# A norm's transposed rows kept in PSUM until VectorE splits them, and a normalisation cut at column 511

## The chip, the cores and the metric

The kernel runs on one core of a Trainium2 chip. The metric is device time in microseconds (us), taken as a median over runs. The engines are TensorE (PE, with its weight loads PEld), VectorE (DVE), ScalarE (ACT), GpSimd (POOL), and SyncE (SP), which issues the transfers. They read and write SBUF, the large on-chip memory, and PSUM, where matmuls accumulate in banks of 512 float32 columns.

## The reference

Two transformer-like layers run over 512 tokens, 256 of them context and 256 latent, with rows of 1024 numbers (D). Layer 0 mixes tokens by a gated delta rule, layer 1 by differential attention; a gated feed-forward network (SwiGLU) follows each. Every one of the four sub-layers is closed by a norm over a row:

```
x = LN(alpha * x + gate * sublayer(x * (1 + scale) + shift))
LN(x) = (x - mean(x)) * rsqrt(mean((x - mean(x))^2) + 1e-5) * g + b
```

`gate`, `scale` and `shift` come from a condition vector and are constant over the tokens of a stream. Only the latent half of the result is returned.

## The kernel before

**Tiles.** The 512 tokens are four tiles `t` of 128 rows (0 and 1 context, 2 and 3 latent). `x` (named `big` in the profile) holds a tile with tokens on the 128 partitions and 1024 columns. A matmul needs the features on the partitions, so each normalised tile is transposed by PE in eight blocks of 128 x 128.

**Products.** All products are made from float32 values that are split in two parts: a rounded one (`hh` of activations, `wh` or `wxh` of weights) and the rest (`hl`, `wl`, `wxl`). Each product is three matmuls: hi x hi, hi x lo, lo x hi (`mm3`). The rest is value minus rounded value, an instruction with two sources (`tt`, line 410), which DVE or POOL may do. The rounded part is a cast by ACT (`cp`, line 424) or DVE (line 425).

**A norm.** `resid` (from line 1417) adds a sub-layer's output, times its gate, to `x` and collects statistics (`bn_stats`, line 1430). `norm` (line 1433) turns them into mean and 1/sqrt by a chain of small operations on one column (`sm`), and writes the normalised row to `n`: DVE takes columns 0 to 511 (`ts`, line 416), ACT 512 to 1023 (`act`, line 437), in parallel. `ln` (line 1450) then starts two threads `to_hT` (line 1458), one for each half row `b`:

1. four transposes of `n` into a PSUM bank `pt` (line 463; banks `wb`, `wc`, `o`);
2. four scale-and-shift operations, out of `pt` into an SBUF buffer `hfb` of 512 columns (named `w` in the profile, as the buffers of the feed-forward network are), each on DVE or ACT; the bank is then free;
3. `hh`, the cast of `hfb`, on ACT or DVE;
4. `hl`, `hfb` minus `hh`, on POOL or DVE; the buffer is then free.

The matmuls of the next sub-layer take `hh` and `hl` from there. A third thread, `ln_x`, multiplies `n` by g and adds b on POOL (`big<-n,lnr`, `big<-big,lnr`), for the next residual.

Three sets of norms go through `to_hT`: LN0 (behind the layer-0 mixer, four tiles, about 465 to 490 us of the span), LN1 (behind the layer-0 feed-forward network, four tiles, about 840 to 873) and LN2 (behind the attention, tiles 2 and 3, about 1069 to 1097). That makes 10 norms and 20 half rows. The last norm of the kernel goes straight to the output and is not touched.

**Order.** No order is written by hand. A planner (class `Sched`) runs when the kernel is built: every thread is a generator with a rank, and each operation gets a planned start from a cost model (`cost`, line 396) and from the engine, buffers and events it needs. `Alt` offers an operation to two engines; the planner takes the one that would end first, with a penalty on DVE set by `spare` (`LNW`, line 76). `shared` (line 404) marks operations that the planner lets exclude each other between DVE and POOL: all of POOL's, and those of DVE with no PSUM source and either two sources or more than one column out. Where it plans PE idle for over 1 us, `warm` (line 526) puts in matmuls on a tile of ones. Each engine runs its list in order.

Of the kernel before, what the change touches and what calls it, by code (L numbers as in the profile page):

```python
# [13 lines left out]
ALU = mybir.AluOpType  # L14
# [360 lines left out]
def trunk_kernel(ctx: ExitStack, tc: tile.TileContext, A: dict, out: bass.AP, dbg=None, stop=None):  # L375
# [11 lines left out]
    def fs(ap):  # L387
        n = 1
        for s in ap.shape[1:]:
            n *= s  # L390
        return n

    isps = lambda *a: any(x.space == PSUM for x in a)
    isap = lambda x: not isinstance(x, (int, float)) and x is not None

    def cost(e, out, srcs, scal=(), one=False):
        n, p = fs(out), sum(1 for x in scal if isap(x))
        if e == "v":
            return ((n / 2 if one and not isps(out, *srcs) else n) + 66 + 58 * p) / 0.96
        if e == "s":  # L400
            return 0.833 * n + (50 if isps(*srcs) else 93) + 93 * p
        return 259 + 3.33 * n if p else 150 + (0.84 * n + 180 if one else 2.1 * n)

    def shared(op, srcs, out=None):

        op.port = op.eng == "g" or (op.eng == "v" and not isps(*srcs) and (len(srcs) > 1 or not isps(out) and fs(out) > 1))
        return op

    def tt(o, a, b, op, e="v"):
        return shared(Op(e, cost(e, o, (a, b)), lambda: E[e].tensor_tensor(o, a, b, op), o, a, b), (a, b))  # L410

    def tta(o, a, b, op):
        return Alt([tt(o, a, b, op, "v"), tt(o, a, b, op, "g")])

    def ts(o, a, s1, s2, o0, o1=None, e="v"):
        f = lambda: E[e].tensor_scalar(o, a, s1, s2, o0, o1) if o1 is not None else E[e].tensor_scalar(o, a, s1, s2, o0)  # L416
        return shared(Op(e, cost(e, o, (a,), (s1, s2), True), f, o, a), (a,), o)

    def stt(o, a, s, b, o0, o1):
        return shared(Op("v", cost("v", o, (a, b), (s,)), lambda: V.scalar_tensor_tensor(o, a, s, b, o0, o1), o, a, b), (a, b))  # L420
# [6 lines left out]
    def cpa(o, a):  # L427
        return Alt([cp(o, a, "s"), cp(o, a, "v")])

    def act(o, a, f, scale=1.0, bias=None, accum=None):  # L430
        kw = {}
        if bias is not None:
            kw["bias"] = bias
        if accum is not None:
            kw["accum_out"] = accum
        c = cost("s", o, (a,), (scale, bias)) + (95 if accum is not None else 0)
        return Op("s", c, lambda: S.activation(o, a, f, scale=scale, **kw), o, a)  # L437

    def spare(alt, wait):

        for op in alt:
            if op.eng == "v":
                op.wait = wait
        return alt

    def dve(o, n, f, *aps):
        return Op("v", (n + 66) / 0.96, f, *aps)
# [13 lines left out]
    def tr(o, a):  # L461
        k = a.shape[0]
        return Op("pe", 110.0, lambda: T.transpose(o, a, ident[0:k, 0:k]), o)  # L463
# [52 lines left out]
    hl = const([P, KT, 512], "hl", F32R)  # L516
    hhf = hh.bitcast(F32)
# [25 lines left out]
    def event(*k):  # L543
        e = ev.setdefault(k, Event())
        e.name = k
        return e
# [15 lines left out]
    def rsqrt(x, n):  # L562

        yb = yield Alloc(SM)
        hb = yield Alloc(SM)
        mb = yield Alloc(SM)
        y, xh, m = yb[:, 0:n], hb[:, 0:n], mb[:, 0:n]
        yield ts(y.bitcast(I32), x.bitcast(I32), 1, None, ALU.logical_shift_right)
        yield Par([ts(y.bitcast(I32), y.bitcast(I32), -1, 0x5F3759DF, ALU.mult, ALU.add),
                   ts(xh, x, -27.0 / 1024.0, None, ALU.mult)])  # L570

        if n == 1:

            zb = yield Alloc(SM)
            z = zb[:, 0:1]
            yield ts(m, y, y, x, ALU.mult, ALU.mult)
            yield ts(z, m, -10.0 / 3.0, m, ALU.add, ALU.mult)
            yield ts(m, z, 5.0, y, ALU.add, ALU.mult)
            yield ts(z, m, m, xh, ALU.mult, ALU.mult)
            yield ts(y, z, 9.0 / 16.0, m, ALU.add, ALU.mult)  # L580
            yield Free(hb, mb, zb)
            return yb
        yield tt(m, y, y, ALU.mult)
        yield tt(m, m, x, ALU.mult)
        yield stt(m, m, -10.0 / 3.0, m, ALU.add, ALU.mult)
        yield stt(y, m, 5.0, y, ALU.add, ALU.mult)
        yield tt(m, y, y, ALU.mult)
        yield tt(m, m, xh, ALU.mult)
        yield stt(y, m, 9.0 / 16.0, y, ALU.add, ALU.mult)
        yield Free(hb, mb)  # L590
        return yb
# [748 lines left out]
    n = 0  # L1340
# [92 lines left out]
    def norm(i, t, stats, done):  # L1433

        yield Wait(*done)
        mv = yield Alloc(SM)
        yield dve(mv, 12, lambda: V.bn_aggr(mv[:, 0:2], stats[:, 0:2, :]))
        yield ts(mv[:, 1:2], mv[:, 1:2], 1e-5, None, ALU.add)
        rs = yield from rsqrt(mv[:, 1:2], 1)
        n = yield Alloc(TNN)  # L1440
        x = xs["x"]
        a, b = slice(0, 512), slice(512, 1024)
        nb = mv[:, 2:3]
        yield ts(nb, mv[:, 0:1], -1.0, rs[:, 0:1], ALU.mult, ALU.mult)
        yield Par([ts(n[:, a], x[:, t, a], mv[:, 0:1], rs[:, 0:1], ALU.subtract, ALU.mult),
                   act(n[:, b], x[:, t, b], AF.Identity, rs[:, 0:1], nb)])
        yield Free(mv, rs, stats)
        return n

    def ln(i, t, stats, done, keep):  # L1450
        n = yield from norm(i, t, stats, done)
        left = [2 + keep]
        for b in range(2):
            spawn(to_hT(i, t, b, n, left), RK_LN + (RK_T[t] if i == 2 else t))
        if keep:
            spawn(ln_x(i, t, n, left), RK_LNX[i] + t)

    def to_hT(i, t, b, n, left):
        r = 1 if t < 2 else 0
        ab = yield Wait(event("fold", i))  # L1460
        w_ = LNW3[i] if t == 3 else LNW[i]
        pt = yield Alloc(*YP)
        hfb = yield Alloc(W5)
        hf = hfb.t.rearrange("p (j n) -> p j n", j=4)
        if i < 2 and t < 3:
            yield Later(LN_SLACK)
        for j in range(4):
            kt = 4 * b + j
            yield tr(pt[:, P * j:P * j + P], n[:, P * kt:P * kt + P])
        ops = []  # L1470
        for j in range(4):
            kt = 4 * b + j
            o, p, sa, sb = hf[:, j, :], pt[:, P * j:P * j + P], ab[:, 0, kt, r:r + 1], ab[:, 1, kt, r:r + 1]
            ops.append(spare(Alt([ts(o, p, sa, sb, ALU.mult, ALU.add), act(o, p, AF.Identity, sa, sb)]), w_[0]))
        yield Par(ops)
        yield Free(pt)
        c, k4 = slice(P * t, P * t + P), slice(4 * b, 4 * b + 4)
        yield spare(cpa(hh[:, k4, c], hf), w_[1])
        yield spare(tta(hl[:, k4, c], hf, hhf[:, k4, c], ALU.subtract), w_[2])
        yield Free(hfb)  # L1480
        left[0] -= 1
        if left[0] == 0:
            yield Free(n)
        yield Set(event("hTb", i, t, b))
        if used(("hT", i, t), 2):
            yield Set(event("hT", i, t))
        if used(("fold", i), 8 if i < 2 else 4):
            yield Free(ab)
# [13 lines left out]
    def used(k, n):  # L1502

        seen[k] = seen.get(k, 0) + 1
        return seen[k] == n
# [633 lines left out]
    LNR, TNN, W5 = xt("lnr", [P, 2, D], 1), xt("n", [P, D], 2), xt("w5", [P, 512], NW5)  # L2139
# [174 lines left out]
```

## Time and profile before

| | |
|---|---|
| median of 3 runs | 1284.76 us (1284.17 to 1285.11) |
| the profiled execution, device time | 1284.39 us |
| span in its profile | 1282.6 us |
| mean granted PE clock | 0.994 |
| PE busy | 1239.9 us, 97% |
| DVE busy | 891.3 us, 69% |
| ACT busy | 575.8 us, 45% |
| POOL busy | 322.5 us, 25% |

The span runs from the first to the last instruction; the device time holds 1.8 us around it. A row such as `L416 DVE TENSOR_SCALAR n<-big,sm,sm` is an instruction of line 416 on DVE, which writes `n` from `big` and two scalars `sm`; buffer numbers are left out. Times are us unless marked ns. What stands in square brackets is how long the engine was idle before an instruction, and what released it.

### The profile page before, as it was taken

How to read it: one execution, taken by the hardware profiler on the slowest of the kernel's cores; microseconds unless marked ns; L12 is line 12 of the kernel's file. 1: busy time of each engine (PE TensorE's matmuls, PEld its weight loads, DVE VectorE, ACT ScalarE, POOL GpSimd, SP SyncE). 2: the span in 40 equal slices, each digit the busy share in tenths (PEclk: the TensorE clock that was granted, in tenths of full speed). 3: DMA queues.
4: the chain of work that ended last, by engine and by line, in shares of the span. 5: the costliest groups of instructions: out<-in, count | busy, mean ns of one | idle time of the engine just before them, and what ended most of it. 6: DMA issues, size and time to landing. Idle time of an engine off the chain costs nothing.

```text
span 1282.6 us, 24147 instructions
## 1 busy us (share of the span) xinstructions
PE 1239.9 (97%) x9576; PEld 1018.9 (79%) x9576; DVE 891.3 (69%) x2036; ACT 575.8 (45%) x1295; POOL 322.5 (25%) x190
## 2 busy tenths in 40 slices
PE   9999899999999999999999999999999998999997
PEld 6576678788787787888888888879878866999986
DVE  3298859698783776888378562475998978655546
ACT  2258657667644435222112322145545444444431
POOL 0013212123222148222101123134122236322200
PEclk9999999999999999999999999999999999999999
DMA  9423312011111743555256563224223155755550
GB/s 367 150 78 137 133 43 76 19 51 51 35 51 61 252 140 133 196 174 180 97 172 209 189 198 104 81 85 144 91 87 124 53 200 182 237 188 184 181 181 33
DMA packets 54753, 171.58 MB, mean 134 GB/s; under 512 B 5744, under 2 KB 14064, under 8 KB 53872
## 3 DMA queue, kind: packets, MB, share of 16 engines
q1 hardware_dynamic: 54640, 170.04, 39.6%
q8 instruction: 75, 1.23, 0.4%
q14 instruction: 38, 0.31, 0.1%
HBM read 168.97 MB, written 1.05 MB: 133 GB/s over the span
## 4 chain that ended last, share of the span: by engine, by line
PE 77%; DVE 15%; ACT 5%; issue 2%; DMA 0%; DVEq 0%; SPq 0%
PE pj L459 32%; PE wa L459 18%; PE wc L459 11%; PE wb L459 6%; PE o L459 6%; DVE acc L420 2%; DVE sm L416 1%; DVE sm L420 1%; PE pj L536 1%; ACT jk L437 1%; PE wc L463 1%; DVE sm L410 1%; DVE hl L410 1%; DVE wl L410 1%; ACT N L424 1%
## 5 line engine op out<-in xcount | busy, mean ns | idle before, releaser
L424 ACT CAST wh<-w 128x1024 fp32r<-128x1024 f32 (+1 forms) x131 | 136.9, 1046 | 207.5 <-PE wa L459 54.8
L459 PE MATMUL pj<-hl,wh 128*128 128x512 f32 (+1 forms) x592 | 219.3, 371 | 0.0
L459 PE MATMUL pj<-hh,wh 128*128 128x512 f32 (+1 forms) x592 | 218.1, 368 | 0.6 <-DVE acc L420 0.6
L410 POOL TENSOR_TENSOR wl<-w,wh 128x1024 fp32r<-128x1024 f32 (+1 forms) x40 | 97.3, 2432 | 385.7 <-ACT wh L424 337.1
L459 PE MATMUL pj<-hh,wl 128*128 128x512 f32 (+1 forms) x512 | 187.5, 366 | 0.0
L459 PEld LDWEIGHTS pj<-hh,wh 128*128 128x128 f32 x592 | 112.5, 190 | 15.7 <-issue 1.1
L459 PEld LDWEIGHTS pj<-hl,wh 128*128 128x128 f32 x592 | 112.2, 190 | 14.5 <-issue 0.7
L410 DVE TENSOR_TENSOR wl<-w,wh 128x1024 fp32r<-128x1024 f32 x52 | 63.5, 1222 | 64.1 <-ACT wh L424 62.7
L459 PEld LDWEIGHTS pj<-hh,wl 128*128 128x128 f32 x512 | 97.3, 190 | 10.6 <-issue 0.2
L459 PE MATMUL wa<-hl,wh 128*128 128x256 f32 (+2 forms) x288 | 96.5, 335 | 0.0
L459 PE MATMUL wa<-hh,wh 128*128 128x256 f32 (+2 forms) x288 | 96.0, 334 | 0.0
L420 DVE SCALAR_TENSOR_TENSOR adaE<-w,sT,adaE 128x512 f32<-128x512 f32 x89 | 73.2, 859 | 5.3 <-DMA w<-in_adaw_dram 4.7
L424 ACT CAST wh<-wx 128x1024 fp32r<-128x1024 f32 x36 | 37.8, 1049 | 58.0 <-PE pj L459 28.1
L420 DVE SCALAR_TENSOR_TENSOR acc<-pj,cst,acc 128x510 f32<-128x510 f32 (+1 forms) x80 | 59.3, 742 | 5.9 <-ACT acc L437 5.0
L459 PE MATMUL wa<-hh,wxl 128*128 128x512 f32 (+1 forms) x176 | 61.7, 350 | 0.0
L459 PE MATMUL pj<-hh,wxl 128*128 128x512 f32 (+1 forms) x176 | 60.9, 346 | 0.0
L459 PEld LDWEIGHTS wa<-hh,wh 128*128 128x128 f32 (+1 forms) x288 | 54.4, 189 | 6.0
L459 PEld LDWEIGHTS wa<-hl,wh 128*128 128x128 f32 (+1 forms) x288 | 54.0, 188 | 6.0
L410 POOL TENSOR_TENSOR hidl<-w,hidh 128x512 fp32r<-128x512 f32 x20 | 29.2, 1462 | 108.1 <-ACT hidh L424 108.1
L410 POOL TENSOR_TENSOR wxl<-w,wh 128x1024 fp32r<-128x1024 f32 x13 | 31.5, 2428 | 82.1 <-ACT wh L424 50.5
L459 PE MATMUL wa<-hh,wl 128*128 128x256 f32 (+2 forms) x152 | 49.9, 328 | 0.0
L410 POOL TENSOR_TENSOR h1l<-fth,h1h 128x256 fp32r<-128x256 f32 x20 | 29.4, 1472 | 77.8 <-ACT h1h L424 77.8
(664 smaller groups left out, 3242.8 us busy)
## 6 DMA issues: line engine op xcount, KB each, us to landing
w<-in_adaw_dram SPq DMA_DIRECT2D x71, 512.0 KB, 4.2
w<-in_wgu_dram SPq DMA_DIRECT2D x59, 512.0 KB, 4.5
w<-in_wd_dram SPq DMA_DIRECT2D x31, 512.0 KB, 3.8
w<-in_wdn_dram SPq DMA_DIRECT2D x26, 512.0 KB, 3.8
wx<-in_adaw_dram SPq DMA_DIRECT2D x17, 512.0 KB, 3.9
w<-in_wo_dram SPq DMA_DIRECT2D x15, 512.0 KB, 4.9
wx<-in_wgu_dram SPq DMA_DIRECT2D x15, 512.0 KB, 4.2
wx<-in_wd_dram SPq DMA_DIRECT2D x10, 512.0 KB, 3.9
```

What stands on the lines that cost most here:

```text
L410: return shared(Op(e, cost(e, o, (a, b)), lambda: E[e].tensor_tensor(o, a, b, op), o, a, b), (a, b))
L416: f = lambda: E[e].tensor_scalar(o, a, s1, s2, o0, o1) if o1 is not None else E[e].tensor_scalar(o, a, s1, s2, o0)
L420: return shared(Op("v", cost("v", o, (a, b), (s,)), lambda: V.scalar_tensor_tensor(o, a, s, b, o0, o1), o, a, b), (a, b))
L424: return Op("s", cost("s", o, (a,)), lambda: S.copy(o, a), o, a)
L437: return Op("s", c, lambda: S.activation(o, a, f, scale=scale, **kw), o, a)
L459: return Op("pe", c, lambda: T.matmul(o, lhsT=l, rhs=r, start=start, stop=stop), o)
L463: return Op("pe", 110.0, lambda: T.transpose(o, a, ident[0:k, 0:k]), o)
L536: T.matmul(t[:, 0:P], lhsT=ones, rhs=ones, start=True, stop=True)
```

## The change

`to_hT` no longer takes the SBUF buffer. The scale-and-shift operations write back into the PSUM bank, in place. `hh` is cast from the bank and `hl` is computed from the bank and `hh`, now always on DVE (before, 16 of the 20 were on POOL and 4, those of LN2, on DVE). The bank is freed after `hl`. `norm` cuts a row at column 511, so DVE does 511 columns and ACT 513. The planner's cost model takes a DVE operation with one SBUF source as twice as fast, and as excluding POOL, only where its width is even.

```diff
@@ cost, shared
-            return ((n / 2 if one and not isps(out, *srcs) else n) + 66 + 58 * p) / 0.96
+            return ((n / 2 if one and n % 2 == 0 and not isps(out, *srcs) else n) + 66 + 58 * p) / 0.96
...
-        op.port = op.eng == "g" or (op.eng == "v" and not isps(*srcs) and (len(srcs) > 1 or not isps(out) and fs(out) > 1))
+        op.port = op.eng == "g" or (op.eng == "v" and not isps(*srcs) and (len(srcs) > 1 or not isps(out) and fs(out) % 2 == 0))
@@ norm
-        a, b = slice(0, 512), slice(512, 1024)
+        a, b = slice(0, 511), slice(511, 1024)
@@ to_hT
         pt = yield Alloc(*YP)
-        hfb = yield Alloc(W5)
-        hf = hfb.t.rearrange("p (j n) -> p j n", j=4)
+        hf = pt.t.rearrange("p (j n) -> p j n", j=4)
...
         yield Par(ops)
-        yield Free(pt)
         c, k4 = slice(P * t, P * t + P), slice(4 * b, 4 * b + 4)
         yield spare(cpa(hh[:, k4, c], hf), w_[1])
-        yield spare(tta(hl[:, k4, c], hf, hhf[:, k4, c], ALU.subtract), w_[2])
-        yield Free(hfb)
+        yield tt(hl[:, k4, c], hf, hhf[:, k4, c], ALU.subtract)
+        yield Free(pt)
```

The order of every engine is the same up to the first norm of LN0. Behind it the planner lays it out anew. DVE's weight splits go from 143 to 144 and POOL's from 62 to 61. What follows are rows of the lists of before and of the changed kernel; a number behind a name is the buffer's, and means nothing across kernels.

**LN0, DVE, the norm chain of tile 1** (`sm` are the one-column operations, `wa` and `pj` products of the layer-0 output). Before:

```order
L416 TENSOR_SCALAR sm_5991<-sm_5989,sm_5979 128x1
L416 TENSOR_SCALAR sm_6001<-sm_5991 128x1
L416 TENSOR_SCALAR sm_5991<-sm_6001,sm_5989 128x1
L416 TENSOR_SCALAR sm_6001<-sm_5991,sm_5990 128x1
L416 TENSOR_SCALAR sm_5989<-sm_6001,sm_5991 128x1
L416 TENSOR_SCALAR sm_5979<-sm_5979,sm_5989 128x1
L416 TENSOR_SCALAR n_6015<-big_5681,sm_5979,sm_5989 128x512
L410 TENSOR_TENSOR wa_5734<-wa_5734,gate_5686 128x512
```

and after:

```order
L416 TENSOR_SCALAR sm_5991<-sm_5989,sm_5979 128x1
L410 TENSOR_TENSOR hl<-wc_5957,hh 128x4x128
L416 TENSOR_SCALAR sm_6000<-sm_5991 128x1
L416 TENSOR_SCALAR sm_5991<-sm_6000,sm_5989 128x1
L416 TENSOR_SCALAR sm_6000<-sm_5991,sm_5990 128x1
L416 TENSOR_SCALAR sm_5989<-sm_6000,sm_5991 128x1
L410 TENSOR_TENSOR hl<-wb_5958,hh 128x4x128
L416 TENSOR_SCALAR sm_5979<-sm_5979,sm_5989 128x1
L416 TENSOR_SCALAR n_6018<-big_5681,sm_5979,sm_5989 128x511
L410 TENSOR_TENSOR pj_5961<-pj_5961,gate_5686 128x512
```

Both `hl` of tile 0 now stand inside the chain that ends in tile 1's `n`. The chains of tiles 2 and 3 hold the two `hl` of the tile before them in the same way, so six are ahead of tile 3's `n`; tile 3's two scale-and-shift operations on DVE stand behind its `n`, where two of tile 2 stood ahead of it. POOL's list there loses its eight `hl`, and has `wxl`, `wxl`, `big<-n` of tile 2, `wl` and `big<-big` in a row behind the additions of tile 1.

**LN1, DVE, the end of the chain of tile 2.** Before:

```order
L416 TENSOR_SCALAR sm_8925<-sm_8918,sm_8917 128x1
L416 TENSOR_SCALAR sm_8916<-sm_8925,sm_8918 128x1
L416 TENSOR_SCALAR sm_8903<-sm_8903,sm_8916 128x1
L410 TENSOR_TENSOR wxl_8898<-wx_8575,wxh_8897 128x1024
L416 TENSOR_SCALAR n_8943<-big_5681,sm_8903,sm_8916 128x512
L410 TENSOR_TENSOR wa_8673<-wa_8673,gate_6514 128x512
```

and after:

```order
L416 TENSOR_SCALAR sm_8902<-sm_8894 128x1
L410 TENSOR_TENSOR hl<-wb_8861,hh 128x4x128
L416 TENSOR_SCALAR sm_8894<-sm_8902,sm_8892 128x1
L416 TENSOR_SCALAR sm_8902<-sm_8894,sm_8893 128x1
L425 CAST hh<-wc_8862 128x4x128
L416 TENSOR_SCALAR sm_8892<-sm_8902,sm_8894 128x1
L410 TENSOR_TENSOR hl<-wc_8862,hh 128x4x128
L416 TENSOR_SCALAR sm_8881<-sm_8881,sm_8892 128x1
L416 TENSOR_SCALAR n_8928<-big_5681,sm_8881,sm_8892 128x511
L410 TENSOR_TENSOR wa_8665<-wa_8665,gate_6472 128x512
```

The split `wxl` ahead of tile 2's `n` is gone from DVE, and two `hl` of tile 1 stand in the chain. The same place in POOL's list, with the first splits of the attention's weights (`wl_8642` and `wxl_8653` of before are `wl_8634` and `wxl_8645` of after), before:

```order
L410 TENSOR_TENSOR wl_8642<-w_8394,wh_8641 128x1024
L410 TENSOR_TENSOR wxl_8653<-w_8432,wxh_8652 128x1024
L410 TENSOR_TENSOR hl<-w_45_8801,hh 128x4x128
L410 TENSOR_TENSOR hl<-w_46_8803,hh 128x4x128
L410 TENSOR_TENSOR hl<-w_47_8871,hh 128x4x128
L410 TENSOR_TENSOR hl<-w_48_8873,hh 128x4x128
L410 TENSOR_TENSOR wl_8914<-w_8655,wh_8913 128x1024
L410 TENSOR_TENSOR big_5681<-n_8943,lnr_6312 128x1024
L410 TENSOR_TENSOR hl<-w_50_8976,hh 128x4x128
```

and after:

```order
L410 TENSOR_TENSOR wl_8634<-w_8386,wh_8633 128x1024
L410 TENSOR_TENSOR wxl_8645<-w_8424,wxh_8644 128x1024
L410 TENSOR_TENSOR wxl_8886<-w_8567,wxh_8885 128x1024
L410 TENSOR_TENSOR wxl_8907<-w_8647,wh_8906 128x1024
L410 TENSOR_TENSOR wl_8923<-w_8684,wh_8922 128x1024
L410 TENSOR_TENSOR big_5681<-n_8928,lnr_6261 128x1024
L410 TENSOR_TENSOR wxl_8948<-w_8697,wh_8947 128x1024
L410 TENSOR_TENSOR big_5681<-big_5681,lnr_6261 128x1024
```

Four `hl` are gone from between the weight splits, and two `wxl` stand there.

**LN2, DVE, from tile 2's `n` on** (`wb` and `wc` are attention outputs of tile 3 that go into its residual, `o` is the bank of tile 2's transposes). Before:

```order
L416 TENSOR_SCALAR n_11266<-big_5681,sm_11229,sm_11239 128x512
L416 TENSOR_SCALAR w_77_11282<-wc_11281,fab_8330 128x128 x4
L420 SCALAR_TENSOR_TENSOR big_5681<-big_5681,wb_10918 128x512
L420 SCALAR_TENSOR_TENSOR big_5681<-big_5681,wc_10966 128x512
L1430 BN_STATS bst_11198<-big_5681 128x6 x2
L1437 BN_AGGR sm_11324<-bst_11198 128x2
L416 TENSOR_SCALAR sm_11324<-sm_11324 128x1
L416 TENSOR_SCALAR sm_11328<-sm_11324 128x1
L416 TENSOR_SCALAR sm_11328<-sm_11328 128x1
L416 TENSOR_SCALAR sm_11329<-sm_11324 128x1
L410 TENSOR_TENSOR hl<-w_76_11280,hh 128x4x128
L410 TENSOR_TENSOR hl<-w_77_11282,hh 128x4x128
```

and after:

```order
L416 TENSOR_SCALAR n_11254<-big_5681,sm_11211,sm_11220 128x511
L416 TENSOR_SCALAR o_11262<-o_11262,fab_8322 128x128 x4
L410 TENSOR_TENSOR wb_10926<-wb_10926,gate_10238 128x512
L410 TENSOR_TENSOR hl<-o_11262,hh 128x4x128
L420 SCALAR_TENSOR_TENSOR big_5681<-big_5681,wb_10926 128x512
L410 TENSOR_TENSOR wc_10964<-wc_10964,gate_10238 128x512
L1430 BN_STATS bst_11193<-big_5681 128x6
L420 SCALAR_TENSOR_TENSOR big_5681<-big_5681,wc_10964 128x512
L1430 BN_STATS bst_11193<-big_5681 128x6
L410 TENSOR_TENSOR hl<-o_11288,hh 128x4x128
L1437 BN_AGGR sm_11324<-bst_11193 128x2
```

Before, both `hl` of tile 2 stand behind the residual and inside the chain of tile 3, one after the other. Now one stands ahead of the residual's additions and one at their end. PE's list at this place had 52 matmuls on ones (26 of them twice over) between tile 2's transposes and its first matmul; now it has 6 between the transposes of tile 2's two halves, which both use bank `o`. Of the 24 matmuls of tile 2's `gate_up_tok` (line 1645, the first half of the feed-forward network for one tile), 12 stood ahead of tile 3's transposes, and 22 do now.

## The prediction

> **What bounds the kernel now.** I read the page first: busy times, then the chain that ended last.
>
> ```profile
> PE 1239.9 (97%) x9576; PEld 1018.9 (79%) x9576; DVE 891.3 (69%) x2036; ACT 575.8 (45%) x1295; POOL 322.5 (25%) x190
> PE 77%; DVE 15%; ACT 5%; issue 2%; DMA 0%; DVEq 0%; SPq 0%
> ```
>
> PE is busy for 97% of the span and makes most of the chain, so a change on DVE and POOL can pay only where PE stands idle, fills time with matmuls on `ones`, or runs at a low clock. The second view, engines by stretch (start:end, length, then busy PE, PEld, DVE, ACT, POOL, granted clock, DMA share, GB/s), tells where.
>
> ```profile
> 500.00:840.00 340.00, 340.00 (x1511) 279.24 (x1510) 215.23 (x288) 89.02 (x110) 71.87 (x38) 1.00 0.49 162
> 840.00:872.00 32.00, 29.25 (x152) 25.28 (x150) 26.05 (x69) 17.56 (x38) 12.80 (x8) 0.89 0.17 50
> 1062.00:1100.00 38.00, 31.59 (x190) 25.00 (x189) 30.88 (x63) 17.51 (x30) 22.07 (x10) 1.00 0.55 175
> ```
>
> Between 500 and 840 us PE has no idle time at all: a new order there is worth nothing. The stretches around the second set of norms (LN1, 840 to 872) and the third (LN2, 1062 to 1100) are short of work, and at LN1 the clock falls too. Third, what PE waits for in those stretches, and in 872 to 900 (us in total, times, longest):
>
> ```profile
> PE wc L459 <- DVE wxl L410: 2.7, 1, 2.7
> PE wc L463 <- ACT n L437: 0.7, 1, 0.7
> PE o L463 <- DVE n L416: 4.0, 2, 2.2
> PE pj L459 <- DVE hl L410: 1.5, 2, 1.1
> ```
>
> Every one is the end of a chain through a norm or a split. Fourth, the groups behind them (of the first: busy us, mean ns | idle before; of the others: min/median/max ns, first and last start):
>
> ```profile
> L410 POOL TENSOR_TENSOR hl<-w,hh 128x512 fp32r<-128x512 f32 x16 | 21.3, 1344 | 31.6 <-DVE sm L416 19.9 <-ACT hh L424 11.4 <-DVE hh L425 0.4
> L416 DVE TENSOR_SCALAR n<-big,sm,sm x10: 533/539/1424, 467.3 to 1084.1; 128x512 f32<-128x512 f32 x10
> L437 ACT ACTIVATE n<-big,sm,sm x10: 812/816/852, 467.4 to 1084.2; 128x512 f32<-128x512 f32 x10
> ```
>
> The 16 hl on POOL, 1.34 us each, go to DVE. DVE's half of a norm takes 0.54 us alone, but up to 1.42. The reason is seen in the timelines (start, length):
>
> ```profile
> 850.94 1.42 DVE L416 TENSOR_SCALAR n<-big,sm,sm 128x512 f32<-128x512 f32 x1
> 850.78 1.30 POOL L410 TENSOR_TENSOR hl<-w,hh 128x512 fp32r<-128x512 f32 x1 [0.24 <-ACT hh L424]
> 473.43 0.68 DVE L410 TENSOR_TENSOR wa<-wa,gate 128x512 f32<-128x512 f32 x1
> 473.19 2.71 POOL L410 TENSOR_TENSOR hl<-w,hh 128x512 fp32r<-128x512 f32 x2
> 850.00 1.02 DVE L416 TENSOR_SCALAR sm<-sm,sm 128x1 f32<-128x1 f32 x4
> ```
>
> The first: n issued 0.16 us behind a POOL split ends at 852.36, 0.28 after it; it was held. The second: a DVE operation of two sources, one in PSUM (`wa`), runs its 0.68 us right through two POOL splits. The third: four operations of one column each run at 0.26 beside POOL. So what is held is DVE work from SBUF with two sources, or with one source and an even width.
>
> **The change, part by part.**
>
> *LN2.* Here both parts of the change meet.
>
> ```profile
> 1074.37 1.14 ACT L424 CAST hh<-w 128x512 fp32r<-128x512 f32 x2
> 1076.95 2.38 POOL L410 TENSOR_TENSOR wl<-w,wxh 128x1024 fp32r<-128x1024 f32 x1
> 1079.27 2.85 POOL L410 TENSOR_TENSOR wxl<-wy,wh 128x1024 fp32r<-128x1024 f32 x1
> 1077.81 4.85 DVE L410 TENSOR_TENSOR hl<-w,hh 128x512 fp32r<-128x512 f32 x2
> 1084.07 0.54 DVE L416 TENSOR_SCALAR n<-big,sm,sm 128x512 f32<-128x512 f32 x1
> 1087.56 2.39 POOL L410 TENSOR_TENSOR big<-big,lnr 128x1024 f32<-128x1024 f32 x1
> 1087.68 3.42 DVE L410 TENSOR_TENSOR hl<-w,hh 128x512 fp32r<-128x512 f32 x2
> 1072.17 0.63 PE L463 MATMUL o<-cst,n 128*128 128x128 f32 x4 [1.84 <-DVE n L416]
> 1073.07 5.97 PE L536 MATMUL pj<-ones 128*128 128x128 f32 x52
> 1084.66 0.66 PE L463 MATMUL o<-cst,n 128*128 128x128 f32 x4 [2.18 <-DVE n L416]
> 1090.55 0.49 PE L459 MATMUL pj<-wh,hl 128*128 128x512 f32 x1 [1.10 <-DVE hl L410]
> 1096.82 0.39 PE L459 MATMUL pj<-wh,hl 128*128 128x512 f32 x1
> 1097.05 0.28 PE L459 MATMUL pj<-hh,wh 128*128 128x256 f32 x1
> ```
>
> Two pairs of hl on DVE take 4.85 and 3.42 us, each beside POOL work. From PSUM, like `wa` above, a pair takes 2 x 0.68 = 1.36. The first pair stands ahead of tile 3's n, which so comes 3.49 earlier, less 0.24 for the odd width (below) and some 0.45 that the first hl now waits for its transposes and cast in the middle of the row: n is 2.8 earlier. PE filled 5.97 us with 52 matmuls on `ones` while it had nothing to do; in the new order 22 matmuls of tile 2's gate_up, not 12, come ahead of tile 3's transposes. These 10, at the 0.23 us between the last two rows, move 2.3 us of work into the wait. The second pair is 2.06 shorter, of which PE waited 1.10 (at 1090.55); I count 0.7, since hl still comes one cast behind hh. Sum: 2.8 + 2.3 + 0.7 = 5.8 earlier; the last phase starts at about 1091.2 for 1097.05. What is late next is tile 3's n again, at some 1081.5. Bounds: -2.8 (no more than the n) to -8.
>
> *LN1.* The planner sends the split wxl from DVE to POOL, and eight hl the other way.
>
> ```profile
> 858.59 3.42 DVE L410 TENSOR_TENSOR wxl<-wx,wxh 128x1024 fp32r<-128x1024 f32 x1
> 858.55 2.37 POOL L410 TENSOR_TENSOR wl<-w,wh 128x1024 fp32r<-128x1024 f32 x1
> 862.66 0.41 PE L459 MATMUL wc<-wxh,hh 128*128 128x256 f32 x1
> 862.87 0.41 PE L459 MATMUL wc<-wxl,hh 128*128 128x256 f32 x1
> 868.36 0.28 PE L459 MATMUL wc<-wl,hh 128*128 128x256 f32 x1
> 868.48 0.28 PE L459 MATMUL wc<-wh,hl 128*128 128x256 f32 x1
> ```
>
> wxl lost to POOL's wl, PE stood 2.7 us, and from 862.1 to about 868.2 matmuls of this shape took 0.41 and started 0.21 apart (first two rows), where they later take 0.28 and start 0.12 apart (last two). That is 6.1 us x (1 - 0.12 / 0.21), about 2.7 lost to the clock. Removed: 2.7 + 2.7, and the 0.7 of the wait for n. Put back: eight hl of 0.68 now stand in DVE's norm chains, ahead of n. I walked DVE's and PE's new rows by hand with these durations, and PE then waits for n three times: 1.8, 0.7 and 1.35, together 3.85, each too short to lower the clock (the 1.84 and 2.18 at LN2 left it at 1.00). Net -2.3. Bounds: -6.1, if DVE's idle time takes in all eight, to +0.3, if all their 5.4 and four odd halves (4 x 0.24) come on the path.
>
> *LN0.* This is the place that loses.
>
> ```profile
> 481.17 0.70 DVE L410 TENSOR_TENSOR pj<-pj,gate 128x512 f32<-128x512 f32 x1 [0.74 <-PE pj L459]
> 481.85 0.73 DVE L416 TENSOR_SCALAR w<-wc,fab 128x128 f32<-128x128 f32 x2
> 486.25 0.97 DVE L416 TENSOR_SCALAR n<-big,sm,sm 128x512 f32<-128x512 f32 x1
> 488.20 1.28 PE L536 MATMUL pj<-ones 128*128 128x128 f32 x10
> ```
>
> POOL's hl hid there beside a full PE. Now six hl (4.07 us) and four odd halves (0.96) come ahead of the end of tile 3's n. Against them: n is no longer held (0.43), DVE's idle 0.74 fills, and the two affines (0.73) go behind n. n ends 4.07 + 0.96 - 0.43 - 0.74 - 0.73 = 3.1 later. PE had about 1.0 us of filling from 488.20 to its next real matmul; that cover is used up and 2.1 is left. Bounds: 0 to +4.5.
>
> *The width 511.* No row has an odd width above one. Its time is at least 0.54, the row at 512, if odd changes nothing. If each column needs a step of its own: an operation of one column takes 0.26 (1.02 / 4), which leaves 0.28 of the 0.54 for 256 steps of two columns, so 511 steps make 0.26 + 0.56 = 0.82; `wa` with 512 steps and no pointer operands took 0.68. I take 0.78, between these and nearer to the row that is worked out from n itself, so 0.24 more than now. For its hold the bounds are none (like the odd width of one) and a whole POOL operation (2.4). And I take no hold: of the two properties of n, its parity is what the change alters, and the only odd rows are not held. The nearest row by size says the reverse, so this is the weakest term, and the main rival below is built on it. ACT's 513th column is one in 512 of 0.816 us: nothing. Column 511 makes the fourth transpose wait for ACT's half as well, but ACT ends no later than a DVE half of 0.78 plus three transposes of 0.15.
>
> A rule of the Trainium skill speaks against my choice: "VectorE: DVE Perf Modes", in its walkthrough of the pipeline (mode 2x_2P), says that an operation with one SBUF source takes both ports when its outermost count is even, or odd and equal in source and destination. Source and destination here both have 511, so by that rule n stays fast and is still held; no trace so far shows which, and the sum by it is that of the first rival.
>
> *The rest.* hh read from PSUM by ACT: nothing, it is one pass either way. A PSUM bank held two splits longer (1.3 us): at LN2 the second half of tile 2 waits for bank `o`, which is in the 5.8. Behind LN1 the attention stage gets a new order, with no work added: 0, give or take 1.5.
>
> Sum: 2.1 - 2.3 - 5.8 = -6.0. The profiled execution took 1284.39 us, 0.37 less than the median of 1284.76; so 1278.4 against it, 1278.8 against the median.
>
> **Rivals.**
>
> *The odd half is still held.* Then the planner, which now takes n as free of the port, has put POOL's long operations beside it. n runs 0.54, so each is 0.24 shorter, but at LN0 the n of tiles 2 and 3 stand beside POOL's wxl and wl or big: with 1.2 to 2.4 each on the path, 2.1 becomes about 5.4. At LN1 tile 2's n stands beside the moved wxl: +1.8, and another 2.7 if PE's idle time lowers the clock as at 862; -2.3 becomes -0.5 to +2.2. At LN2 tile 3's n stands beside wl: -5.8 becomes -3.9. Sum +1.0 to +3.7: 1286 to 1288.5, same or slower. It decides from a mean hold of some 1.5 us on these four n. For it: the 1.42 row, nearest by size. Against: the one-column rows. 25%.
>
> *DVE becomes the bound.* hl stands in an in-order queue in the middle of a norm chain and needs hh, an ACT cast of about 0.57 (half of 1.14). If each of the six hl at LN0 waits 0.6, n of tile 3 is 3.6 later still; at LN1 three such add 1.8. Sum -0.6: about 1284, no change. For it: DVE is busy 26 of 32 us at LN1 already. Against: the chains' small operations are laid around the casts. 16%.
>
> *The change doesn't do what it says*: hl from PSUM is held by POOL all the same, at 2 us for each of twenty. The `wa` row speaks against that. Then it is slower, 1290 or so. 4%.
>
> **How the numbers follow.** My forecast has 55%, and by itself 1276 to 1282 (the LN terms' bounds do not all fall on one side). A difference under 0.2%, 2.6 us, can't be told from none. Faster: 0.88 of the forecast and a quarter of the DVE case, 0.52. Same: 0.06 of the forecast, 0.10 of the DVE case, 0.09 of the held half, 0.01: 0.26. Slower: the rest, 0.22, mostly the held half. The range reaches into the held half: 1275.5 to 1287.5 leaves out some 6% below and 12% above.
>
> **What would show it.** n at 511: about 0.78 and never longer, or 0.54 with some above 1 beside POOL. All twenty hl near 0.68. LN2: no long row of `ones`, the last phase some 5.8 earlier in distance from LN1's end. LN1: no 2.7 us wait for wxl, clock near 1.00. LN0: a new PE wait for n of about 2. If LN0 and LN1 lose more than 4 us together, or n is held, I am wrong.

## The result, and the profile after

| | median, us | runs | ratio to before, 95% interval |
|---|---|---|---|
| before | 1284.76 | 5 (1281.38 to 1285.19) | |
| changed | 1292.81 | 5 (1289.06 to 1293.02) | 1.0057 (1.0037 to 1.0076) |
| changed, once more | 1291.10 | 6 (1289.03 to 1292.97) | 1.0052 (1.0035 to 1.0068) |

The second row of the changed kernel was taken beside a later run of before, whose median there was 1284.28 (23 runs). The change makes the kernel 0.5 to 0.6% slower, some 7 to 8 us, where 1278.8 was forecast. It lies outside the forecast's range and on the other side; the first rival, an n that is still held, names the cause. The profiled execution took 1291.21 us.

The page of the changed kernel: POOL has lost the 16 hl, PE is busy for as long as before, in a longer span.

```profile
PE 1241.3 (96%) x9538; PEld 1019.5 (79%) x9538; DVE 892.3 (69%) x2048; ACT 580.3 (45%) x1297; POOL 300.0 (23%) x176
```

The groups answer the two questions that the forecast left (first row min/median/max ns; the others busy us, mean ns | idle before):

```profile
L416 DVE TENSOR_SCALAR n<-big,sm,sm x10: 541/937/2605, 468.9 to 1093.2; 128x511 f32<-128x511 f32 x10
L410 DVE TENSOR_TENSOR hl<-o,hh 128x512 fp32r<-128x512 f32 x7 | 4.8, 688 | 3.6 <-ACT hh L424 3.6
L410 DVE TENSOR_TENSOR hl<-wc,hh 128x512 fp32r<-128x512 f32 x7 | 4.8, 689 | 1.2 <-ACT hh L424 1.2
L410 DVE TENSOR_TENSOR hl<-wb,hh 128x512 fp32r<-128x512 f32 x6 | 4.1, 688 | 0.7 <-ACT hh L424 0.6
```

All twenty hl take 0.69: from PSUM, nothing holds them. But n of 511 columns takes 0.54 where it is alone, the same as 512, and up to 2.6: it runs as fast as 512, and it is still held. The timelines of tile 3 at LN0 and at LN1 (DVE, POOL, PE; start, length, [idle before]):

```profile
492.86 2.60 DVE L416 TENSOR_SCALAR n<-big,sm,sm 128x511 f32<-128x511 f32 x1
492.84 2.34 POOL L410 TENSOR_TENSOR big<-big,lnr 128x1024 f32<-128x1024 f32 x1
495.52 1.12 PE L463 MATMUL o<-cst,n 128*128 128x128 f32 x4 [4.48 <-DVE n L416]
878.31 2.32 DVE L416 TENSOR_SCALAR n<-big,sm,sm 128x511 f32<-128x511 f32 x1
878.01 2.34 POOL L410 TENSOR_TENSOR wxl<-w,wh 128x1024 fp32r<-128x1024 f32 x1 [0.29 <-ACT wh L424]
880.78 1.09 PE L463 MATMUL o<-cst,n 128*128 128x128 f32 x4 [4.40 <-DVE n L416]
```

At LN0 POOL started 0.02 us ahead, and n ended 0.28 behind POOL's end. PE then stood 4.5 and 4.4 us, and its transposes took 1.12 and 1.09 where they take 0.66 at the full clock. The stretches of 450 to 500 and 872 to 900 us (columns as in the prediction) show it: clock 0.97 and 0.94, and 43.6 us of 50 busy where the kernel before had 48.9.

```profile
450.00:500.00 50.00, 43.61 (x205) 35.85 (x204) 37.38 (x84) 23.35 (x47) 28.19 (x12) 0.97 0.37 119
872.00:900.00 28.00, 23.60 (x188) 23.43 (x187) 15.91 (x28) 13.86 (x27) 15.32 (x7) 0.94 0.34 114
```

To see where the time goes I cut each span at four rows: n of tile 0 at LN0 and at LN1, n of tile 2 at LN2, and the first matmul of the last phase (`pj<-hh,wh` of 256 columns behind LN2). For the kernel before they are the first three rows here and 1097.05 above, for the changed one the next four:

```profile
467.33 0.54 DVE L416 TENSOR_SCALAR n<-big,sm,sm 128x512 f32<-128x512 f32 x1
845.25 0.54 DVE L416 TENSOR_SCALAR n<-big,sm,sm 128x512 f32<-128x512 f32 x1
1071.48 0.54 DVE L416 TENSOR_SCALAR n<-big,sm,sm 128x512 f32<-128x512 f32 x1
...
468.91 0.54 DVE L416 TENSOR_SCALAR n<-big,sm,sm 128x511 f32<-128x511 f32 x1
854.15 0.54 DVE L416 TENSOR_SCALAR n<-big,sm,sm 128x511 f32<-128x511 f32 x1
1079.89 1.02 DVE L416 TENSOR_SCALAR n<-big,sm,sm 128x511 f32<-128x511 f32 x1
1103.53 0.28 PE L459 MATMUL pj<-hh,wh 128*128 128x256 f32 x1
```

The differences of these starts, for all runs below (one profiled execution each; in the last row the two last stretches are left as one number; "no hold" and the other names are explained with the experiments):

| us between | start, LN0 | LN0, LN1 | LN1, LN2 | LN2, last phase | last phase, end | span |
|---|---|---|---|---|---|---|
| before | 467.3 | 377.9 | 226.2 | 25.6 | 185.6 | 1282.6 |
| changed | 468.9 | 385.2 | 225.7 | 23.6 | 185.9 | 1289.4 |
| changed, once more | 467.8 | 385.5 | 226.2 | 25.8 | 185.9 | 1291.2 |
| 511, rules of before | 467.1 | 381.6 | 222.4 | 24.5 | 185.2 | 1280.7 |
| PSUM, 512 | 467.2 | 382.9 | 224.2 | 24.8 | 185.3 | 1284.4 |
| 511 alone | 469.3 | 380.7 | 230.9 | 29.3 | 185.3 | 1295.5 |
| no hold, ACT 1023 | 468.6 | 384.6 | 220.7 | 23.7 | 186.0 | 1283.6 |
| no hold, 511 left out | 468.7 | 383.2 | 220.8 | 21.8 | 187.9 | 1282.3 |
| PSUM at LN1, LN2 | 468.0 | 377.9 | 221.2 | 27.6 | 185.1 | 1279.8 |
| PSUM at LN2 | 467.5 | 377.9 | 224.9 | 21.3 | 185.5 | 1277.1 |
| PSUM at LN0 | 468.8 | 382.8 | 221.4 | 25.5 | 185.6 | 1284.1 |
| PSUM at LN0, no hold | 467.4 | 378.8 | 223.1 | 25.2 | 185.6 | 1280.1 |
| hl on DVE from SBUF | 467.0 | 383.8 | 224.9 | 211.1 | | 1286.8 |

The first column is the same list of instructions in every kernel; its 467.0 to 469.3 is a difference between executions (the changed kernel has 468.9 and 467.8), and no part of the change's effect. Nor is a profiled execution always near the median of its runs: that of 511 with the rules of before took 1282.51 us, the fastest of 12 and 4.7 under their median, and that of PSUM at LN0 1286.19, 1.7 above. So a microsecond between two rows of this table is a hint and no more.

### The profile page after: what moved, and what is told of

Same layout as the page of the kernel before. It is cut to its first block, busy times and chain, and to the rows that moved or that the text cites. A ratio compares the mean times of both kernels' runs of the same rounds, so it can differ in the third digit from the quotient of the medians.

```text
span 1289.4 us, 24080 instructions
## 1 busy us (share of the span) xinstructions
PE 1241.3 (96%) x9538; PEld 1019.5 (79%) x9538; DVE 892.3 (69%) x2048; ACT 580.3 (45%) x1297; POOL 300.0 (23%) x176
## 3 DMA queue, kind: packets, MB, share of 16 engines
q8 instruction: 75, 1.23, 0.4%
## 5 line engine op out<-in xcount | busy, mean ns | idle before, releaser
L459 PE MATMUL pj<-hh,wh 128*128 128x512 f32 (+1 forms) x648 | 234.3, 362 | 0.6 <-DVE acc L420 0.6
L459 PE MATMUL pj<-hl,wh 128*128 128x512 f32 (+1 forms) x648 | 234.4, 362 | 0.0
L420 DVE SCALAR_TENSOR_TENSOR adaE<-w,sT,adaE 128x512 f32<-128x512 f32 x112 | 91.0, 855 | 5.8 <-DMA w<-in_adaw_dram 5.3
L424 ACT CAST wxh<-w 128x1024 fp32r<-128x1024 f32 x40 | 42.0, 1049 | 68.2 <-PE pj L459 21.5
L459 PE MATMUL wa<-hl,wh 128*128 128x512 f32 (+2 forms) x176 | 60.4, 343 | 0.0
L459 PE MATMUL wa<-hh,wh 128*128 128x512 f32 (+2 forms) x176 | 60.2, 342 | 0.0
L410 DVE TENSOR_TENSOR wxl<-w,wh 128x1024 fp32r<-128x1024 f32 x24 | 30.3, 1266 | 31.4 <-ACT wh L424 31.3
L459 PE MATMUL wa<-hh,wxh 128*128 128x256 f32 (+1 forms) x152 | 51.1, 336 | 0.0
L459 PE MATMUL wa<-hl,wxh 128*128 128x256 f32 (+1 forms) x152 | 50.8, 334 | 0.0
L410 POOL TENSOR_TENSOR wxl<-w,wxh 128x1024 fp32r<-128x1024 f32 x10 | 24.1, 2413 | 100.2 <-ACT wxh L424 54.1
```

Source lines behind the costliest of these rows:

```text
L424: return Op("s", cost("s", o, (a,)), lambda: S.copy(o, a), o, a)
L459: return Op("pe", c, lambda: T.matmul(o, lhsT=l, rhs=r, start=start, stop=stop), o)
```

## The experiments

**1. 511 columns with the planner's rules of before**, and **2. 512 columns with the rows in PSUM.** In 1 `cost` and `shared` are those of before, which are the true ones (an odd width is held); 2 is

```diff
-        a, b = slice(0, 511), slice(511, 1024)
+        a, b = slice(0, 512), slice(512, 1024)
```

> The changed kernel with the planner's cost and exclusion rules of before: 511 columns stay, but the planner counts n as twice as fast and as excluding POOL. Theory H (n at 511 is held by POOL like n at 512, and the loss comes from the planner's belief that it is not): POOL's long splits no longer stand beside n, the PE waits for n at LN0 and LN1 (4.5, 1.9, 4.4, 2.3 us in the changed kernel) shrink to under 2 each, time 1279 to 1283 us. Rival Q (the six to eight hl in DVE's in-order chains, which wait for ACT's hh, are what costs): 1288 or more, waits for n as long as they are. Rival P (scale-and-shift written back into PSUM is slower, and the bank is held longer): 1286 to 1290.

> The changed kernel with the row cut at 512 again; the planner's rules are those of the change, which at an even width are those of before. Its instruction order is the same as that of the kernel with 511 and the rules of before, so the two differ in the width alone. H: same time as that one within 0.2%, n at 512 takes 0.54 us alone like 511. If odd did change the hold or the rate, n would take about 0.78 there and never longer, and the two would differ.

Measured: 1287.18 us for 511, ratio 1.0019 (1.0003 to 1.0035), and 1285.84 for 512, 1.0008 (0.9995 to 1.0022), 12 runs each. The two have the same order on every engine and differ in the width alone; in both, the n's of LN0's tile 2 and LN1's tile 3 are held alike (at LN1 with the POOL row that holds them):

```profile
483.65 2.63 DVE L416 TENSOR_SCALAR n<-big,sm,sm 128x511 f32<-128x511 f32 x1
874.36 2.58 DVE L416 TENSOR_SCALAR n<-big,sm,sm 128x511 f32<-128x511 f32 x1
874.32 2.33 POOL L410 TENSOR_TENSOR big<-big,lnr 128x1024 f32<-128x1024 f32 x1
...
483.80 2.64 DVE L416 TENSOR_SCALAR n<-big,sm,sm 128x512 f32<-128x512 f32 x1
875.69 2.58 DVE L416 TENSOR_SCALAR n<-big,sm,sm 128x512 f32<-128x512 f32 x1
875.65 2.33 POOL L410 TENSOR_TENSOR big<-big,lnr 128x1024 f32<-128x1024 f32 x1
```

So the parity changes neither rate nor hold. By the ratios, telling the planner so takes away 4 to 6 us of the loss. But I expected 1279 to 1283, and the two are no faster than before: even the true rules don't keep POOL off n (2.6 at LN0 still), and keeping the rows in PSUM in all three sets is worth nothing in sum. The 1287.18 lies in the range of rival P (1286 to 1290, a slower PSUM path); experiments 3 and 6 speak against P as the cause of the loss.

**3. 511 and the new rules in the kernel before**, rows through SBUF, hl with POOL or DVE.

> The kernel before with only the cut at 511 and the planner's new rules; the normalised rows go through SBUF and hl stays with POOL or DVE as before. H: n is held by POOL's hl, splits and products where the planner now puts them side by side; PE waits for n appear, 1286 to 1289 us. Q and P: neither hl nor PSUM has changed, so 1284.8 within 0.2% (1282.2 to 1287.4), with no new wait for n.

Measured: 1296.18 us, ratio 1.0089 (1.0069 to 1.0109): more than the 1286 to 1289 expected, and slower than the changed kernel, which has the PSUM part too. n is held here too, at LN1's tile 2 by POOL's wl, which started 1.04 us ahead of it:

```profile
866.64 2.60 DVE L416 TENSOR_SCALAR n<-big,sm,sm 128x511 f32<-128x511 f32 x1
865.60 3.36 POOL L410 TENSOR_TENSOR wl<-wx,wh 128x1024 fp32r<-128x1024 f32 x1
```

The cut with its rules costs 11 us by itself, and with the rows in PSUM less, so the loss doesn't come from PSUM. But most of these 11 us are not PE's waits for n. From 460 to 1215 us they come to 5.5 us, 4.7 in the kernel before (15.5 in the changed kernel); for the n above PE waited only 0.16. The longest, 2.3, is at LN0. The rest lies in the order that the planner makes by the new rules, with other waits (1.9 for `w5l` behind LN2, for example) and stretches at a lower clock (0.97 from 460 to 510 us), and is not taken apart.

**4. The changed kernel's order, with ACT doing 1023 columns of n:**

```diff
-        yield Par([ts(n[:, a], x[:, t, a], ...), act(n[:, b], x[:, t, b], ...)])
+        dv.fn = lambda: V.tensor_scalar(n[:, 0:1], x[:, t, 0:1], ...)
+        sc.fn = lambda: S.activation(n[:, 1:1024], x[:, t, 1:1024], ...)
```

> The order of the changed kernel, row for row, but DVE normalises one column (one column was never held) and ACT the other 1023, which takes ACT about 0.82 + 511 x 0.83 ns = 1.24 us: n is ready some 0.45 later than an n of 0.78 would be, and never held. H: what is left over before is the forecast's sum without the hold plus ten times up to 0.45 on the path: 1281 to 1285 us, waits for n at LN0 4.5 -> about 3, at LN1 4.4 -> under 3, clock at LN1 near 1.00. Q: 1290 or more. P: 1287 or more.

Measured: 1285.66 us, ratio 1.0005 (0.9993 to 1.0018), 0.7 above what H gave, below P and far from Q. But LN0 to LN1 is 384.6, hardly less than the changed kernel's 385.2: with ACT busy for 1.24 per n, hl waited longer for its hh (1.4 us twice). So this run mixes two things, and experiment 9 takes them apart.

**5 to 7. PSUM and DVE for a part of the norms only**, 512 columns and the rules of before:

```diff
+        inps = i > 0        # 5: LN1 and LN2;  6: i == 2;  7: i == 0
+        hfb = pt if inps else (yield Alloc(W5))
...
+        if inps: yield tt(hl[:, k4, c], hf, hhf[:, k4, c], ALU.subtract)
+        else: yield spare(tta(hl[:, k4, c], hf, hhf[:, k4, c], ALU.subtract), w_[2])
```

> The kernel before (512 columns, its rules) with the rows kept in PSUM and split by DVE at LN1 and LN2 alone; at LN0 they go through SBUF and POOL as before. Theory R (keeping them in PSUM loses at LN0, where hl waits for ACT's hh in DVE's queue and delays the next n, and gains behind it): from the stretches of the run with all three at 512, LN0 costs +4.9, LN1 with the attention -2.0 and LN2 -0.8, and of the run without the hold -5.5 and -1.8; so 1278 to 1282.5 us, the stretch from LN0's first n to LN1's first n within 0.5 of the 377.9 of before. Rival S (the differences by stretch are only a new order's chance): 1283 to 1289.

> The kernel before with PSUM and DVE at LN2 alone. There hl was on DVE before, too, so only its source moves. R: hl takes 0.69 for the 2.4 of before, LN2's first n to the last phase 23.5 to 24.8 us for 25.6, time 1282.5 to 1284.5. My forecast's 5.8 at LN2 would give 1279. S: 1284.8 give or take 2.

> The kernel before with PSUM and DVE at LN0 alone. R: LN0's first n to LN1's first n takes 381 to 383.5 us for 377.9; tile 3's n stands behind six hl, each of which waits 0.2 to 1.4 us for ACT; time 1288 to 1290.5. S: 1284.8 give or take 2.

Measured: LN1 and LN2 1280.94 us, ratio 0.9980 (0.9968 to 0.9993); LN2 alone 1279.23, 0.9964 (0.9950 to 0.9977); LN0 alone 1284.47, 1.0003 (0.9991 to 1.0015). LN2 alone is faster than both kernels. Its order is that of before up to LN2, so it shows what PSUM does there (DVE, POOL, PE):

```profile
1074.18 0.69 DVE L410 TENSOR_TENSOR hl<-o,hh 128x512 fp32r<-128x512 f32 x1 [0.27 <-ACT hh L424]
1074.79 0.68 DVE L410 TENSOR_TENSOR hl<-wc,hh 128x512 fp32r<-128x512 f32 x1
1073.46 2.39 POOL L410 TENSOR_TENSOR big<-big,lnr 128x1024 f32<-128x1024 f32 x1
1080.20 0.63 DVE L416 TENSOR_SCALAR n<-big,sm,sm 128x512 f32<-128x512 f32 x1
1071.93 2.40 PE L536 MATMUL pj<-ones 128*128 128x128 f32 x20
1077.33 1.95 PE L536 MATMUL pj<-ones 128*128 128x128 f32 x16
1083.21 1.50 PE L536 MATMUL wa<-ones 128*128 128x128 f32 x12
1091.61 0.28 PE L459 MATMUL pj<-hh,wh 128*128 128x256 f32 x1
```

The pair of hl beside POOL takes 1.37 for 4.85, tile 3's n comes 9.86 behind tile 2's for 12.59, and the last phase starts 21.3 behind tile 2's n for 25.6. That is 4.3 of the 5.8 that I gave LN2. (The 1279.23 looks like the 1279 that 5.8 would give, but before took 1283.78 on that chip, so it is 4.6.) The row of 5.97 us of ones is down to 2.40, but two more rows of ones stand behind it, 48 matmuls in all for 52: what is gone is waiting, since PE's waits in 1062 to 1100 us fall from 6.4 us to 2.8. I expected less (23.5 to 24.8), from the runs with all three sets, and that was wrong. The run with LN1 and LN2 came out as R gave it, but in it LN2 got another order and gave 2 us away: both of its n's are held, at 2.71 and 2.41. LN0 alone loses its 4.9 there as expected, in its profiled execution, but the time is not R's 1288 to 1290.5; it is the 1284.8 of rival S. I did not expect that the loss would be given back: LN1 to LN2 is 4.9 shorter although nothing was changed there. In the new order PE waits 0.5 for wxl at LN1, not 2.7.

**8. All hl on DVE, from SBUF** (`tta` replaced by `tt`, buffer kept).

> The kernel before with all twenty hl on DVE, but from SBUF as before: two SBUF sources. If PSUM as a source is what frees hl of POOL (as the row of wa, 0.68 beside POOL, says), hl shows rows of 1.4 to 2.9 here, the planner lays POOL and DVE one behind the other, and it takes 1287 to 1292 us. If the source doesn't matter, it takes as long as the run with PSUM at 512 (1285.8 give or take 1.5).

Measured: 1290.20 us, ratio 1.0043 (1.0028 to 1.0057). The group's mean is nearly double that of hl from PSUM:

```profile
L410 DVE TENSOR_TENSOR hl<-w,hh 128x512 fp32r<-128x512 f32 x20 | 24.1, 1229 | 2.5 <-ACT hh L424 2.5
```

Against 1285.84 with PSUM: for hl on DVE, the source, with the order that the planner makes for it, is worth some 4 us.

**9 and 10. No hold, and ACT as before.** The changed kernel's order (9) and that of PSUM at LN0 alone (10). Both leave out 511 columns of n, so they serve for times alone; 11 is the changed kernel once more:

```diff
+        dv.fn = lambda: V.tensor_scalar(n[:, 511:512], ...)
+        sc.fn = lambda: S.activation(n[:, 512:1024], ...)
-            yield tr(pt[:, P * j:P * j + P], n[:, P * kt:P * kt + P])
+            yield tr(pt[:, P * j:P * j + P], n[:, P * (4 + j):P * (4 + j) + P])
```

> The changed kernel's order, row for row; DVE normalises one column, ACT 512 as before, the other 511 columns are left out (the transposes of the lower half read the upper half, and the product with g reads x), so n is ready when ACT ends, 0.82 us after the chain, and nothing holds DVE there. It takes from the run with ACT's 1.24 us what that cost. H: what is left against the kernel before is the price of six hl in DVE's queue at LN0 (which wait for ACT's hh) and the gains behind it: LN0's first n to LN1's first n 380 to 382.5 us (changed kernel 385.2, before 377.9), LN1's first n to LN2's first n 220 to 222, time 1280 to 1284. If the hold were not what costs at LN0, that stretch stays at 384 or more.

> The same exclusion of the hold in the kernel with PSUM at LN0 alone (order of that kernel, the same columns left out). There tile 2's n was held 2.1 us and tile 3's came 10.7 later than before. H: LN0's first n to LN1's first n 379 to 381 us for 382.8, the clock of 450 to 500 us back at 1.00 for 0.93, time 1281 to 1283.5. If the queue of hl alone costs there: 382 or more, time 1284 or more.

> The changed kernel once more, beside the two above on the same chip. Same as on record: 1289 to 1293.5 us, n of 511 columns held up to 2.6 us. Where LN0's first n starts (468.9 for 467.3 in the order they share) shows whether those 1.6 us come again.

Measured: 1283.08 us, ratio 0.9994 (0.9983 to 1.0005), for the changed order without the hold; 1282.11, 0.9981 (0.9969 to 0.9993), for PSUM at LN0 without it. The hold costs the changed kernel 8.0 us (1291.10 less 1283.08, on the same chip). PE's waits for n tell the same: 15.5 us in the changed kernel, 6.9 here, from 460 to 1215 us. (The run also takes 0.27 us off each of DVE's n and lets POOL's product start earlier, so 8.0 may be a little too much; the run of 4, where ACT's 1.24 us costs something too, gives 6.0 by the ratios.) By stretches 2.0 of it lie at LN0 (385.2 to 383.2) and 4.9 at LN1 (225.7 to 220.8). In the order of PSUM at LN0 it costs 4.1 there in the profiled executions (382.8 to 378.8, with the clock of 450 to 500 us back at 1.00 from 0.93).

LN0 to LN1 with 383.2 is above the 380 to 382.5 that I gave for 9, and 5.3 above before. DVE's queue makes tile 3's n late. Of 9, the six hl of tiles 0 to 2:

```profile
473.57 0.69 DVE L410 TENSOR_TENSOR hl<-wc,hh 128x512 fp32r<-128x512 f32 x1 [0.58 <-ACT hh L424]
475.45 0.69 DVE L410 TENSOR_TENSOR hl<-wb,hh 128x512 fp32r<-128x512 f32 x1 [0.25 <-ACT hh L424]
480.58 0.69 DVE L410 TENSOR_TENSOR hl<-o,hh 128x512 fp32r<-128x512 f32 x1 [0.96 <-ACT hh L424]
482.45 0.69 DVE L410 TENSOR_TENSOR hl<-wc,hh 128x512 fp32r<-128x512 f32 x1 [0.25 <-ACT hh L424]
488.57 0.69 DVE L410 TENSOR_TENSOR hl<-wc,hh 128x512 fp32r<-128x512 f32 x1 [0.99 <-ACT hh L424]
490.45 0.69 DVE L410 TENSOR_TENSOR hl<-wb,hh 128x512 fp32r<-128x512 f32 x1 [0.37 <-ACT hh L424]
```

Ahead of tile 3's n, DVE waits 3.4 us for hh in these six places. That n then starts 23.3 us behind tile 0's, for 18.9 before. But a late n alone is not the loss, as 10 shows. There the same six hl stand in DVE's queue (with 2.1 us of waits) and tile 3's n comes 25.0 behind tile 0's, later still, yet the stretch to LN1 is only 0.9 above before. First 9, then 10, tile 3's n and what PE did:

```profile
491.98 0.27 DVE L1448 TENSOR_SCALAR n<-big,sm,sm 128x1 f32<-128x1 f32 x1
PE o L463 <- ACT n L1449: 2.2, 1, 2.2
450.00:500.00 50.00, 46.38 (x215) 37.39 (x214) 34.40 (x89) 23.99 (x49) 28.43 (x12) 0.97 0.37 117
...
492.35 0.26 DVE L1447 TENSOR_SCALAR n<-big,sm,sm 128x1 f32<-128x1 f32 x1
PE wc L463 <- ACT n L1448: 1.4, 2, 0.9
450.00:500.00 50.00, 47.90 (x224) 38.23 (x223) 36.81 (x94) 24.78 (x51) 28.70 (x12) 1.00 0.36 115
```

In the order of 9, PE has run out of work: it waits 2.2 for tile 3's n, and behind it eight matmuls start 0.43 apart, where they start 0.23 apart at the full clock: 1.6 us. In the order of 10, PE has products to do ahead of tile 3's transposes, waits 0.5 for them (0.9 for tile 2's), and keeps its clock.

## Why the prediction was wrong, step by step

**The width 511: the step that failed.** I had two rows to choose from, 512 columns (fast, held) and one column (never held), called the first the nearest by size and took the second for its parity. Measured: 511 columns take 0.54 and are held, in 1, 3 and the changed kernel, as 512 are in 2. The Trainium skill ("VectorE: DVE Perf Modes", its walkthrough, mode 2x_2P) has odd and equal counts take both ports as even ones do; the 0.54 and the hold at 511 agree with it. I had quoted that rule against my choice and gave it 25%. A row of one column told nothing on odd widths above one; no run here shows why one column is free.

**The price of the hold.** The rival had 7 to 9.7 between its sum and mine; the changed kernel less the one without the hold is 8.0. The sum was right, in part by luck, since its parts were not: I put 3.3 on LN0 and 1.8 to 4.5 on LN1, and it was 2.0 and 4.9. At LN2 I put 1.9. The first profile shows none (23.6 and 185.9 for 21.8 and 187.9), the second 2.0 with n at 2.64 and 2.09.

**The sum without the hold.** I had -6.0; the run without the hold gives -1.2 us (1283.08 for 1284.28; interval -2.2 to +0.6). Hence even the rival's 1286 to 1288.5 was too low. Term by term, from the table's row "no hold, 511 left out":

- LN0 +2.1: measured +5.3. I counted the length of six hl and not that each stands waiting for hh. The second rival had the mechanism and 3.6 for it; measured 3.4. It was a term of the sum, not an alternative to it. With it tile 3's n is 4.4 late, where I had 3.1 (0.96 of that for odd halves that are not there). PE's wait of about 2 for it was right (2.2). What I had put at nothing is what came with it: a wait of 0.8 for tile 2's n and 1.6 us at the lower clock. From the 1.84 and 2.18 at LN2 I took waits of that length, at LN1, as too short to lower the clock; here one of 2.2 was followed by it. And 10 shows that the term hangs on the order: with other work ahead of PE's transposes it is 0.9.
- LN1 -2.3 (with the attention at 0): measured -5.4. I had put back 3.85 us of PE's waits for n; without the hold they are 1.9, in two. Another part was counted too surely, though it came true here: 2.7 for the low clock behind PE's wait for wxl. The run with PSUM at LN2 alone has the same order there and the same wait, yet no low clock:

```profile
PE wc L459 <- DVE wxl L410: 2.7, 1, 2.7
835.00:872.00 37.00, 33.62 (x187) 28.36 (x186) 29.05 (x71) 21.39 (x45) 12.62 (x8) 1.00 0.22 75
```

  The kernel before has 0.91 in that stretch. Whether a stop of 2.7 us costs the clock differs between executions. The rest of the -5.4, which takes in the attention's new order, is not traced.
- LN2 -5.8: measured -3.8 to the start of the last phase, and then +2.3 behind it, where PE waited 1.7 for a split (`w5l`) that DVE does late in this order. Tile 3's n comes 11.3 behind tile 2's for 12.59, so 1.3 earlier and not 2.8; the matmuls on ones are 24 for 52. Where LN2 is changed alone, -4.3 with nothing given back: there n is 2.7 earlier, as I had it, but the 2.3 for work moved into the row of ones did not come, since 48 ones are left. The mechanism (hl freed of POOL, tile 3's n earlier) was right; its size was 1.5 too large. One part is in the traces of the changed kernel (first two rows) and of before: written back into PSUM, four scale-and-shift operations took 1.82 on ACT, where into SBUF they took 1.51. I had put nothing for that. And where I had 0.45 for the wait of the first hl, the second waits 1.91 for its hh.

```profile
1087.78 1.82 ACT L437 ACTIVATE o<-o,fab 128x128 f32<-128x128 f32 x4 [2.33 <-PE o L463]
1090.25 0.69 DVE L410 TENSOR_TENSOR hl<-o,hh 128x512 fp32r<-128x512 f32 x1 [1.91 <-ACT hh L424]
1072.83 1.51 ACT L437 ACTIVATE w<-o,fab 128x128 f32<-128x128 f32 x4 [1.61 <-PE o L463]
```

**hl from PSUM is not held**: right, in all twenty rows, from the one row of `wa`. The Trainium skill ("SBUF — State Buffer", "Who interferes with whom") says that a DVE operation with at most one SBUF input outside the two-port modes does not contend with GpSimd; the 0.69 in all twenty rows here agrees. From SBUF, with two sources there, the mean was 1.23 (experiment 8).

What stays open: how much of the 5.3 at LN0 goes with the waits for hh alone; no run takes that wait away in the same order. Where most of the 11 us of experiment 3 comes from. And why the planner's order behind an unchanged LN1 is 4.9 us better in the run with PSUM at LN0 than before is only in part shown (0.5 of waiting for wxl for 2.7), not as a rule.

## What to carry to other kernels

An edit to a scheduler's model is a claim on the hardware, and it acts at every place that the model decides: here a wrong claim (odd widths don't exclude POOL) cost 4 to 6 us in the changed kernel and 11 us, with the cut, in the kernel before. When two rows bracket an unknown, take the one that shares the mechanism, not the label. And an operation moved into an in-order queue brings its operand's wait along: count length and wait, and then look whether the engine that waits at the end has other work in hand, for that decides what the delay costs (5.3 or 0.9 us at LN0). Keeping the rows in PSUM paid where hl was on DVE already and held by POOL (LN2 alone, 0.36% faster than before), not where POOL's hl had been hidden.

## What the runs showed of the hardware

Scale-and-shift of 128x128 from a PSUM bank takes longer, four in a row, when it writes back into the bank than when it writes to SBUF: ACT 1.82 for 1.51 (rows above), DVE, in the run with PSUM at LN2 alone and in the kernel before, 1.78 for 1.37:

```profile
1072.13 1.78 DVE L416 TENSOR_SCALAR wc<-wc,fab 128x128 f32<-128x128 f32 x4 [1.25 <-PE wc L463]
1073.27 1.37 DVE L416 TENSOR_SCALAR w<-wc,fab 128x128 f32<-128x128 f32 x4 [1.25 <-PE wc L463]
```

DVE's n, with one SBUF source and 0.54 us alone, is held by a POOL operation that started 0.04 us ahead of it for that operation's whole length, at 511 columns as at 512 (2.58 us in both, in experiments 1 and 2).

PE stops of about the same length were followed by a lower clock in some places and not in others: 2.7 us at LN1 in before (0.91 from 835 to 872 us) and in the run with PSUM at LN2 alone (1.00); 2.2 us at LN0 in experiment 9 (0.97 from 450 to 500 us) and at LN2 in before (1.00).
